# The squared-ReLU tiles of a transformer block return through the ring of weight buffers; squares of x^T queue behind q's casts

## The chip, the cores and the metric

The kernel runs on one core of a Trainium2 chip. The metric is the time of one execution in device microseconds (us), as a median of several. The core has TensorE (matmuls), VectorE (DVE), ScalarE (ACT), GpSimd (POOL) and SyncE (SP, which here only issues DMAs); 16 DMA engines move data between DRAM and the on-chip memory SBUF. Matmuls write into eight banks of PSUM.

## The reference, cut to what matters

One encoder block on 512 tokens and 16 learned meta tokens, width 2048, float32:

```python
h = rms_norm(h_res, norm1_g)
proj = h @ w_in                    # [conv B | conv C | conv x | q | k | v], 6 x 1024 columns
y_conv = short_conv_mixer(b_gate, c_gate, u, conv_w, conv_b)
y_attn = neighbourhood_attention(q, k, v, rpb)
mix = concat(rms_norm(y_conv, conv_norm_g), rms_norm(y_attn, attn_norm_g))
h_res = h_res + mix @ w_out
h = rms_norm(h_res, norm2_g)
h_res = h_res + square(relu(h @ w_up)) @ w_down     # 2048 -> 8192 -> 2048
out = rms_norm(h_res, final_norm_g)[:, 16:]
```

## The kernel before

Every float32 operand of a large product is split into two parts, hi (a cast on ACT, L182) and lo (a subtraction on DVE, L183), and each product is three matmuls: hi x hi, hi x lo, lo x hi. Weights come in slabs of 128 x 1024 (512 KB). `load` takes the next buffer of a ring (`wring["raw"]`) and lets SP issue the DMA; `slab` loads and splits into the next buffer of a second ring (`wring["split"]`). A buffer comes free when its last reader is done: a raw one after its lo part, a split one after its last matmul.

The program is written in one order, and a planner, which simulates the engines, lays each engine's instructions into a queue: by program order among those that it expects to be ready. It may move an instruction ahead of earlier ones that wait. On the chip each queue then runs strictly in its order. `tc.issue_after(i)` makes what is issued in its block stand behind `i` in the queue of `i`'s engine; it adds no wait on another engine.

**The start (L229 to L360).** x^T arrives in eight tiles `xTs`, w_in slabs for the first k and v beside it, and q's two slabs `q_raw` behind them. `split_xT` makes `h_hi` and `h_lo` from x^T times the norm's gain, 32 pieces. k and v of the first head pair are projected in two column halves (272 and 256 columns), then q (16 k steps of three 512-column matmuls, into `qps0`). The row sums of x^T squared, for the norm's scale, come from eight squares on ACT (L316) and adds on DVE (L318 to L321), read by ten one-column matmuls (L332), which stand behind q's tenth k step (`q_mid`). From these come `rst`, `diag` and `rs_bc`, whose matmuls (L354) stand behind the third step of the next k. The squares and adds stand behind the last piece of x^T (`hT_last`). The split ring of this stage gives k the first two of wp's three split buffers, and v two others; q0_0, q0_1 and k1_0 then take wp's third, first and second. wp's raw ring has three buffers.

**Up projection (L712 to L793).** 32 groups `n` of 256 hidden columns, each of four steps; a step uses one w_up slab and 42 matmuls. It multiplies in a seven-product scheme whose operands lie in `sobuf` (for the first four of eight places), in `xa_hi`, `xa_lo` and in the xc tiles. `up_out` combines the four banks on ACT and DVE into a tile `e`, one of the two halves of `xq`, applies Relu and Square on ACT, and stores it to DRAM as `a_d[n]` (L779, issued by ACT). The buffers acc0 to acc3 hold temporaries in this stage (`tsum` and the three q tiles), while the residual waits in DRAM as `acc_d`.

**Down projection (L796 to L880).** After the last up group, SBUF is given out anew: `wp2` adds two raw and three split buffers, in the space of `xa_hi` and `xa_lo`, so that the rings have five raw and six split buffers. There are eight chunks of four a tiles (each 128 x 1024, two k steps) and four column blocks `i` of 512 outputs; the last block of the last chunk is done apart (L846 to L867). A block is four slabs of w_down, and each slab feeds 24 matmuls with one a tile; so a block has 96. Each a tile is loaded from `a_d` into one of the two halves of `xq` (`AR`, L806, L819), split into one of seven places of `sobuf` (`A`), and serves all four blocks of its chunk. All four accs come back by GpSimd's queue as soon as their buffers are free (L798); `acc(i, t)` is added to at the end of each block (L840). `gF`, the final gain on all partitions (1 MB), is loaded by SP and read at the end of the last chunk's blocks (L844).

Of the kernel before, what the change touches and what calls it, by code (L numbers as in the profile page):

```python
# [99 lines left out]
def hybrid_block_kernel(  # L100
# [55 lines left out]

    def load(src, name):
        raw = wring["raw"].next(name)
        nc.sync.dma_start(raw, src)
        return raw  # L160

    def part_tiles(name):
        both = wring["split"].next(name)
        return both[:, :SLAB], both[:, SLAB:]
# [4 lines left out]
    def parts(raw, b, name):  # L169
        hi, lo = part_tiles(name)  # L170
        split(hi, lo, raw)
        return (
            hi.rearrange("p (a b) -> p a b", b=b),
            lo.rearrange("p (a b) -> p a b", b=b),
        )

    def slab(src, b, name):
        return parts(load(src, name), b, name)

    def split(hi, lo, src, scale=None):  # L180
        if scale is None:
            nc.scalar.copy(hi, src)  # L182
            nc.vector.tensor_tensor(lo, src, hi.bitcast(F32), op=ALU.subtract)  # L183
        else:
            first = nc.scalar.activation(hi, src, AF.Copy, scale=scale)
            second = nc.vector.scalar_tensor_tensor(
                lo, src, scale, hi.bitcast(F32), op0=ALU.mult, op1=ALU.subtract
            )
            return first, second

    hTp = tc.alloc_tile_pool(name="hTp", bufs=1, side="right")
    h_hi = hTp.tile([P, KT, L], F32R, name="h_hi")
# [36 lines left out]
    with tc.tile_pool(name="p0", bufs=1, side="left") as p0:  # L229
# [45 lines left out]
        def split_xT(i, q):  # L275
            n = ALL[i][0]
            cs = slice(0, n) if i == 0 else slice(L - n, L)
            for k in range(4):
                kt = 4 * q + k
                src = xTs[i][q][:, k * n : (k + 1) * n]  # L280
                both = split(h_hi[:, kt, cs], h_lo[:, kt, cs], src, scale=g1T[:, kt : kt + 1])
            return both

        k0_bank = bank("mm", "mm_k0_1")
        banks = [bank("mm", "mm_k0_0")[:, :272], k0_bank[:, :256]], out_banks(ALL, "v0")
# [8 lines left out]
                for kt in range(4 * q, 4 * q + 4):  # L294
                    project_kt(b[:1], ALL[:1], by_kt(w[a]), kt)
        for q in range(4):
            hT_last = split_xT(1, q)
        for w, b in zip(ws, banks):
            for kt in range(KT):
                project_kt(b[1:], ALL[1:], by_kt(w[kt // PER]), kt)  # L300
# [3 lines left out]
        nc.vector.tensor_copy(par, pg[:, 64:128])  # L304
        wring["split"] = Ring(*split_slots(3, wp))
        (qps0,) = out_banks(REAL, "q0", "aux")
        w_q = [parts(q_raw[a], P, f"q0_{a}") for a in range(2)]
        for kt in range(10):
            q_mid = project_kt([qps0], REAL, w_q[kt // PER], kt)


        sums = []
        with tc.issue_after(hT_last[0].ins), tc.issue_after(hT_last[1].ins):
            for i, (n, _) in enumerate(ALL):
                for q in range(4):
                    nc.scalar.activation(xTs[i][q], xTs[i][q], AF.Square)  # L316
                    if q > 0:
                        nc.vector.tensor_tensor(xTs[i][0], xTs[i][0], xTs[i][q], op=ALU.add)  # L318
                tot = xTs[i][0]
                nc.vector.tensor_tensor(tot[:, : 2 * n], tot[:, : 2 * n], tot[:, 2 * n :], op=ALU.add)  # L320
                nc.vector.tensor_tensor(tot[:, :n], tot[:, :n], tot[:, n : 2 * n], op=ALU.add)  # L321
                sums.append(tot[:, :n])
# [471 lines left out]


    accs = acc_tiles()  # L796
    for g in range(4):
        nc.gpsimd.dma_start(accs[g], acc_d[g])  # L798
    xcp.release()
    xe.release()  # L800
    xap.release()
# [1 line left out]
    wring["raw"] = Ring(*raw_slots(3, wp), *raw_slots(2, wp2))  # L803
    wring["split"] = Ring(*split_slots(3, wp), *split_slots(3, wp2))
    A = Ring(*[lambda name, i=i: part(sobuf, 2048, i) for i in range(7)])
    AR = Ring(*[lambda name, i=i: part(flat(xq), 1024, i) for i in range(2)])  # L806
    pf = ctx.enter_context(tc.tile_pool(name="pf", bufs=1, side="left"))
    gF = pf.tile([P, D], F32, name="gF")
    sq = pf.tile([P, NT, 5], F32, name="sq")
# [4 lines left out]
    turn = 0  # L814
    for ch in range(NCHUNK):
        a_hi, a_lo = [], []
        for n in range(4 * ch, 4 * ch + 4):
            r = AR.next()
            nc.sync.dma_start(r, a_d[n])  # L819
            both = A.next()  # L820
            split(both[:, 0:1024], both[:, 1024:2048], r)
            for b in range(2):
                for lst, c in ((a_hi, 0), (a_lo, 1024)):
                    lst.append([both[:, c + QUART[t // 2, b] * HT + t % 2 * P :][:, :P] for t in range(NT)])
        last = ch == NCHUNK - 1
        k0 = ch * FCH
        if last:
            nc.sync.dma_start(gF, final_g.partition_broadcast(P))
        for i in range(3 if last else 4):
            bs = [bank(tags[turn], f"d{ch}_{i}_{t}") for t in range(NT)]  # L830
            turn ^= 1
            for s_ in range(0, FCH, 2):
                wh, wl = slab(w_down[i, (k0 + s_) // 2], 512, f"dn{ch}_{i}_{s_}")
                for k in range(2):
                    kt = s_ + k
                    for t in range(NT):
                        mm3(bs[t], a_hi[kt][t], a_lo[kt][t], wh[:, k, :], wl[:, k, :], kt == 0, kt == FCH - 1)
            for t in range(NT):
                a = acc(i, t)
                nc.vector.scalar_tensor_tensor(a, bs[t], rs2[:, t : t + 1], a, op0=ALU.mult, op1=ALU.add)  # L840

                if last:
                    nc.scalar.activation(junk[t % 2], a, AF.Square, accum_out=sq[:, t, i : i + 1])
                    nc.vector.tensor_tensor(a, a, gF[:, i * 512 : (i + 1) * 512], op=ALU.mult)  # L844
# [95 lines left out]
```

## Time and profile before

| | us |
|---|---|
| runs of the kernel | 2172.78, 2173.46, 2176.41 (median 2173.46) |
| the profiled execution | 2175.9 |
| its span, first to last instruction | 2174.1 |
| TensorE busy in it | 2148.8 |
| VectorE, ScalarE, GpSimd busy | 1292.1, 798.1, 142.1 |
| mean granted clock of TensorE, as a share of full speed | 0.994 |

A row of a timeline gives an instruction's start and duration in us, its engine, its line in the code, what it writes and reads, its shape, and in brackets how long the engine was idle before it and what ended that. Adjacent like instructions are merged (x7). "SPq" is SP's queue at the moment of a DMA's issue, not the transfer. TensorE's matmuls are pipelined: the time between two starts is what one costs, not the duration shown. The granted clock is 1.00 at 2.4 GHz and near 0.5 at 1.2 GHz.

### The profile page before, as it was taken

Reading aid. Unit: us, or ns where it says so; the run is one execution under the profiler, and the core shown is the slowest. Engines: PE = TensorE matmul, PEld = TensorE weight load, DVE = VectorE, ACT = ScalarE, POOL = GpSimd, SP = SyncE. Lnnn points to the kernel's source line nnn. Section 1 sums busy time; section 2 is a strip of 40 time slices with the busy share of each in tenths; the row PEclk is TensorE's granted clock in tenths of the full one; section 3 lists DMA queues with packets and bytes.
Section 4 is the critical chain, followed back from the end, with each engine's and each line's share of the span. In section 5 each row is a group of like instructions: output and inputs, shape, how many; then the busy total and the mean of one; then the engine's idle time right before and its main releaser. Section 6 shows DMA issues by size and latency. Waiting matters only on the chain.

```text
span 2174.1 us, 33195 instructions
## 1 busy us (share of the span) xinstructions
PE 2148.8 (99%) x13660; PEld 1959.9 (90%) x13660; DVE 1292.1 (59%) x2015; ACT 798.1 (37%) x1110; POOL 142.1 (7%) x260
## 2 busy tenths in 40 slices
PE   9999999999999999999999999998999999999998
PEld 8999999999988889999999999996888888888887
DVE  6776766443435569888888888863434434434334
ACT  5454544222213334554554454442222212222223
POOL 0432311001110000000000000000000000000001
PEclk9999999999999999999999999999999999999999
DMA  5332222222253333433333433365424434333222
GB/s 188 83 93 78 83 83 79 89 96 95 90 165 111 122 126 127 136 127 136 130 134 127 136 134 119 136 260 173 136 98 134 135 98 134 118 114 125 94 87 78
DMA packets 89997, 261.32 MB, mean 120 GB/s; under 512 B 25636, under 2 KB 25716, under 8 KB 88692
## 3 DMA queue, kind: packets, MB, share of 16 engines
q1 hardware_dynamic: 84084, 234.02, 33.0%
q10 hardware_dynamic: 4608, 16.78, 1.9%
q0 software_dynamic: 1152, 8.39, 1.0%
q8 instruction: 107, 1.75, 0.3%
q14 instruction: 46, 0.38, 0.1%
HBM read 233.99 MB, written 25.17 MB: 119 GB/s over the span
## 4 chain that ended last, share of the span: by engine, by line
PE 98%; DMA 1%; ACT 0%; DVE 0%; SPq 0%; issue 0%; ACTq 0%; POOLq 0%; POOL 0%; DVEq 0%
PE d L630 10%; PE d L631 10%; PE d L632 10%; PE u L762 10%; PE u L761 10%; PE u L760 10%; PE mm_v L208 1%; PE mm_v L211 1%; PE mm_v L209 1%; PE mm_k L211 1%; PE mm_k L209 1%; PE mm_k L208 1%; PE mm_u L211 1%; PE mm_c L211 1%; PE mm_q L211 1%; PE mm_u L208 1%
## 5 line engine op out<-in xcount | busy, mean ns | idle before, releaser
L630 PE MATMUL d<-wsp_dn,sobuf 128*128 128x512 f32 x992 | 387.8, 392 | 10.7 <-ACT sobuf L182 8.5
L631 PE MATMUL d<-wsp_dn,sobuf 128*128 128x512 f32 x992 | 387.9, 391 | 0.0
L632 PE MATMUL d<-wsp_dn,sobuf 128*128 128x512 f32 x992 | 384.8, 390 | 0.0
L183 DVE TENSOR_TENSOR wsp_dn<-raw_dn,wsp_dn 128x1024 fp32r<-128x1024 f32 x124 | 151.7, 1224 | 293.0 <-ACT wsp_dn L182 293.0
L182 ACT CAST wsp_dn<-raw_dn 128x1024 fp32r<-128x1024 f32 x124 | 130.5, 1053 | 395.9 <-PE d L632 379.7
L630 PEld LDWEIGHTS d<-wsp_dn,sobuf 128*128 128x128 f32 x992 | 187.3, 189 | 50.5 <-ACT sobuf L182 8.9
L631 PEld LDWEIGHTS d<-wsp_dn,sobuf 128*128 128x128 f32 x992 | 187.4, 189 | 39.2 <-DVE wsp_dn L183 0.2
L632 PEld LDWEIGHTS d<-wsp_dn,sobuf 128*128 128x128 f32 x992 | 186.6, 188 | 38.9
L182 ACT CAST q<-raw_up 128x768 fp32r<-128x768 f32 x128 | 106.8, 834 | 237.3 <-PE u L761 167.3
L183 DVE TENSOR_TENSOR wsp_up<-tsum,wsp_up 128x1024 fp32r<-128x1024 f32 x128 | 156.4, 1222 | 49.7 <-ACT wsp_up L182 45.7
L182 ACT CAST wsp_up<-tsum 128x1024 fp32r<-128x1024 f32 x128 | 134.2, 1049 | 69.5 <-PE u L762 64.7
L760 PE MATMUL u<-sobuf,wsp_up 128*128 128x256 f32 x512 | 145.0, 283 | 0.0
L761 PE MATMUL u<-sobuf,wsp_up 128*128 128x256 f32 x512 | 145.0, 283 | 0.0
L762 PE MATMUL u<-sobuf,wsp_up 128*128 128x256 f32 x512 | 144.6, 283 | 0.0
L183 DVE TENSOR_TENSOR q<-raw_up,q 128x768 fp32r<-128x768 f32 x128 | 122.4, 956 | 34.7 <-ACT q L182 34.6
L761 PE MATMUL u<-sobuf,q 128*128 128x256 f32 x384 | 108.7, 283 | 0.0
L760 PE MATMUL u<-sobuf,q 128*128 128x256 f32 x384 | 108.5, 283 | 0.0
L762 PE MATMUL u<-sobuf,q 128*128 128x256 f32 x384 | 108.5, 283 | 0.0
L840 DVE SCALAR_TENSOR_TENSOR acc<-d,few,acc 128x512 f32<-128x512 f32 x124 | 86.7, 750 | 33.8 <-PE d L632 33.8
L760 PEld LDWEIGHTS u<-sobuf,wsp_up 128*128 128x128 f32 x512 | 98.3, 192 | 0.0
L761 PEld LDWEIGHTS u<-sobuf,wsp_up 128*128 128x128 f32 x512 | 98.3, 192 | 0.0
L762 PEld LDWEIGHTS u<-sobuf,wsp_up 128*128 128x128 f32 x512 | 98.2, 192 | 0.0
(306 smaller groups left out, 5414.9 us busy)
## 6 DMA issues: line engine op xcount, KB each, us to landing
raw_up<-in_w_up_dram SPq DMA_DIRECT2D x128, 512.0 KB
raw_dn<-in_w_down_dram SPq DMA_DIRECT2D x124, 512.0 KB
a_d<-xq ACTq DMA_DIRECT2D x32, 512.0 KB
xq<-a_d SPq DMA_DIRECT2D x32, 512.0 KB
raw_q<-in_w_in_dram SPq DMA_DIRECT2D x16, 512.0 KB
raw_u<-in_w_in_dram SPq DMA_DIRECT2D x16, 512.0 KB
raw_c<-in_w_in_dram SPq DMA_DIRECT2D x16, 512.0 KB
raw_b<-in_w_in_dram SPq DMA_DIRECT2D x16, 512.0 KB
```

The costliest lines, as they stand in the source:

```text
L182: nc.scalar.copy(hi, src)
L183: nc.vector.tensor_tensor(lo, src, hi.bitcast(F32), op=ALU.subtract)
L208: nc.tensor.matmul(b, lhsT=wh, rhs=cols(h_hi, kt), start=kt == 0, stop=False)
L209: nc.tensor.matmul(b, lhsT=wh, rhs=cols(h_lo, kt), start=False, stop=False)
L211: last = nc.tensor.matmul(b, lhsT=wl, rhs=cols(h_hi, kt), start=False, stop=kt == KT - 1)
L630: nc.tensor.matmul(o, lhsT=ah, rhs=wh, start=start, stop=False)
L631: nc.tensor.matmul(o, lhsT=ah, rhs=wl, start=False, stop=False)
L632: nc.tensor.matmul(o, lhsT=al, rhs=wh, start=False, stop=stop)
L760: nc.tensor.matmul(o, lhsT=h, rhs=xh, start=first, stop=False, skip_group_check=True)
L761: nc.tensor.matmul(o, lhsT=h, rhs=xl, start=False, stop=False, skip_group_check=True)
L762: nc.tensor.matmul(o, lhsT=l, rhs=xh, start=False, stop=m == NPR - 1, skip_group_check=True)
L840: nc.vector.scalar_tensor_tensor(a, bs[t], rs2[:, t : t + 1], a, op0=ALU.mult, op1=ALU.add)
```

## The change

Two edits. The squares and adds of x^T now stand behind the second of q's two slab splits (ACT and DVE) instead of behind the last piece of x^T. And in the down projection the a tiles are loaded by `load` into the raw weight ring, each directly ahead of the w_down slab that it is used with, in the first column block of each chunk; the ring `AR` in `xq` is gone. The four acc loads move from GpSimd's queue to SP's, one in each column block of chunk 0, behind the block's second slab. The load of `gF` stands behind the slab issued last before the last chunk.

```diff
     def load(src, name):
         raw = wring["raw"].next(name)
-        nc.sync.dma_start(raw, src)
+        wring["last"] = nc.sync.dma_start(raw, src)
         return raw
...
-        w_q = [parts(q_raw[a], P, f"q0_{a}") for a in range(2)]
+        w_q = []
+        for a in range(2):
+            hi, lo = part_tiles(f"q0_{a}")
+            q_cast = split(hi, lo, q_raw[a])
+            w_q.append(by_kt((hi, lo)))
         for kt in range(10):
             q_mid = project_kt([qps0], REAL, w_q[kt // PER], kt)
...
-        with tc.issue_after(hT_last[0].ins), tc.issue_after(hT_last[1].ins):
+        with tc.issue_after(q_cast[0].ins), tc.issue_after(q_cast[1].ins):
             for i, (n, _) in enumerate(ALL):
                 for q in range(4):
                     nc.scalar.activation(xTs[i][q], xTs[i][q], AF.Square)
...
     accs = acc_tiles()
-    for g in range(4):
-        nc.gpsimd.dma_start(accs[g], acc_d[g])
...
-    AR = Ring(*[lambda name, i=i: part(flat(xq), 1024, i) for i in range(2)])
...
     for ch in range(NCHUNK):
         a_hi, a_lo = [], []
-        for n in range(4 * ch, 4 * ch + 4):
-            r = AR.next()
-            nc.sync.dma_start(r, a_d[n])
-            both = A.next()
-            split(both[:, 0:1024], both[:, 1024:2048], r)
-            for b in range(2):
-                for lst, c in ((a_hi, 0), (a_lo, 1024)):
-                    lst.append([both[:, c + QUART[t // 2, b] * HT + t % 2 * P :][:, :P] for t in range(NT)])
...
         if last:
-            nc.sync.dma_start(gF, final_g.partition_broadcast(P))
+            with tc.issue_after(wring["last"].ins):
+                nc.sync.dma_start(gF, final_g.partition_broadcast(P))
         for i in range(3 if last else 4):
...
             for s_ in range(0, FCH, 2):
+                if i == 0:
+
+                    n = 4 * ch + s_ // 2
+                    both = A.next()
+                    split(both[:, 0:1024], both[:, 1024:2048], load(a_d[n], f"a{n}"))
+                    for b in range(2):
+                        for lst, c in ((a_hi, 0), (a_lo, 1024)):
+                            lst.append([both[:, c + QUART[t // 2, b] * HT + t % 2 * P :][:, :P] for t in range(NT)])
                 wh, wl = slab(w_down[i, (k0 + s_) // 2], 512, f"dn{ch}_{i}_{s_}")
+                if ch == 0 and s_ == 2:
+
+                    with tc.issue_after(wring["last"].ins):
+                        nc.sync.dma_start(accs[i], acc_d[i])
```

`split` now returns its two instructions in both of its branches, and `split_xT` returns nothing.

## Rows read from the trace of the kernel before

**Rows 1.** The page's busy times of the whole span (busy us, share, instructions).

```profile
PE 2148.8 (99%) x13660; PEld 1959.9 (90%) x13660; DVE 1292.1 (59%) x2015; ACT 798.1 (37%) x1110; POOL 142.1 (7%) x260
```

**Rows 2.** TensorE's waits: line, what ended them: us in total, times, longest.

```profile
PE d L630 <- ACT sobuf L182: 8.5, 1, 8.5
PE d L630 <- ACT wsp_dn L182: 2.3, 1, 2.3
PE mm_q L211 <- DVE wsp_q L183: 1.9, 1, 1.9
```

**Rows 3.** ACT's timeline around q's first cast.

```profile
24.37 6.95 ACT L316 ACTIVATE xT<-xT 128x1088 f32<-128x1088 f32 x7
31.22 1.05 ACT L182 CAST wsp_q<-raw_q 128x1024 fp32r<-128x1024 f32 x1
```

**Rows 4.** DVE's timeline: q's first lo part and the last add.

```profile
35.68 1.22 DVE L183 TENSOR_TENSOR wsp_q<-raw_q,wsp_q 128x1024 fp32r<-128x1024 f32 x1
...
41.29 0.42 DVE L321 TENSOR_TENSOR xT<-xT 128x256 f32<-128x256 f32 x1
```

**Rows 5.** TensorE's timeline: last use of k0_0, then q's first matmuls.

```profile
26.45 0.28 PE L211 MATMUL mm_k<-h_hi,wsp_k 128*128 128x256 f32 x1
...
34.30 0.50 PE L208 MATMUL mm_q<-h_hi,wsp_q 128*128 128x512 f32 x1
...
36.95 0.50 PE L211 MATMUL mm_q<-h_hi,wsp_q 128*128 128x512 f32 x1 [1.92 <-DVE wsp_q L183]
...
41.17 0.39 PE L209 MATMUL mm_q<-h_lo,wsp_q 128*128 128x512 f32 x1
```

**Rows 6.** Stretches: length, busy PE, PEld, DVE, ACT, POOL; clock; DMA share; GB/s.

```profile
26.00:28.00 2.00, 2.00 (x20) 2.00 (x19) 1.29 (x1) 2.00 (x3) 0.00 (x0) 1.00 0.00 0
...
37.50:41.20 3.70, 3.70 (x11) 2.85 (x10) 3.70 (x4) 0.00 (x0) 0.00 (x0) 0.54 0.59 173
```

**Rows 7.** TensorE's timeline: first and last d, and a stretch between.

```profile
1452.71 0.40 PE L630 MATMUL d<-wsp_dn,sobuf 128*128 128x512 f32 x1
...
1487.06 0.39 PE L631 MATMUL d<-wsp_dn,sobuf 128*128 128x512 f32 x1
...
1496.58 0.39 PE L631 MATMUL d<-wsp_dn,sobuf 128*128 128x512 f32 x1
...
2142.58 0.39 PE L630 MATMUL dl<-wsp_dlast,sobuf 128*128 128x512 f32 x1
```

**Rows 8.** The chain that ended last, at the head of the down projection: start, us.

```profile
1448.25 11.26 DMA raw_dn<-in_w_down_dram
...
1462.51 7.31 DMA a_d<-xq
1469.88 5.40 DMA xq<-a_d
```

**Rows 9.** Stretches at the head of the down projection, columns as in rows 6.

```profile
1441.00:1452.70 11.70, 11.70 (x99) 11.70 (x99) 3.60 (x3) 3.15 (x3) 1.73 (x4) 1.00 0.97 382
1452.70:1458.00 5.30, 5.30 (x26) 4.34 (x24) 4.19 (x9) 2.85 (x4) 0.00 (x0) 1.00 1.01 414
...
1460.60:1464.40 3.80, 3.78 (x10) 2.92 (x11) 3.31 (x3) 3.76 (x4) 0.00 (x0) 0.55 1.03 428
...
1467.90:1476.40 8.50, 0.05 (x1) 0.00 (x0) 2.47 (x3) 3.13 (x3) 0.00 (x0) 0.69 0.91 361
1476.40:1481.60 5.20, 5.20 (x13) 4.09 (x14) 2.24 (x2) 1.05 (x1) 0.00 (x0) 0.52 0.64 202
```

**Rows 10.** Instructions on acc from 1430 to 1500: issue to landing.

```profile
DMA to landing us min/median/max: 6.1/8.6/9.4
```

**Rows 11.** ACT's timeline: a cast that waited for a load issued at 1476.39.

```profile
1479.49 1.05 ACT L182 CAST sobuf<-xq 128x1024 fp32r<-128x1024 f32 x1 [3.14 <-DMA xq<-a_d]
```

**Rows 12.** SP's timeline: issues of w_down loads.

```profile
1438.14 0.33 SPq L159 DMA_DIRECT2D raw_dn<-in_w_down_dram  x1
...
1445.17 0.33 SPq L159 DMA_DIRECT2D raw_dn<-in_w_down_dram  x1
```

More of the change, by code (lines that the diff above doesn't have):

```diff
@@ L181, in split @@
         if scale is None:
-            nc.scalar.copy(hi, src)
-            nc.vector.tensor_tensor(lo, src, hi.bitcast(F32), op=ALU.subtract)
+            first = nc.scalar.copy(hi, src)
+            second = nc.vector.tensor_tensor(lo, src, hi.bitcast(F32), op=ALU.subtract)
         else:
@@ L188, in split @@
             )
-            return first, second
+        return first, second
     hTp = tc.alloc_tile_pool(name="hTp", bufs=1, side="right")
@@ L280, in split_xT @@
                 src = xTs[i][q][:, k * n : (k + 1) * n]
-                both = split(h_hi[:, kt, cs], h_lo[:, kt, cs], src, scale=g1T[:, kt : kt + 1])
-            return both
+                split(h_hi[:, kt, cs], h_lo[:, kt, cs], src, scale=g1T[:, kt : kt + 1])
         k0_bank = bank("mm", "mm_k0_1")
@@ L296, in hybrid_block_kernel @@
         for q in range(4):
-            hT_last = split_xT(1, q)
+            split_xT(1, q)
         for w, b in zip(ws, banks):
```

## Prediction

> **What bounds the kernel now.** I read four views, in this order. The page's busy times come first: TensorE has work in 2148.8 of 2174.1 us [rows 1], so only its few idle stretches, and the stretches at half clock, can be won. Next comes the list of waits of TensorE. It has seven entries, and three matter here: 8.5 us for a cast into sobuf, 2.3 us for a cast of a w_down slab, 1.9 us for the lo part of q's first slab [rows 2]. The other four are shorter and lie at the very start, which the change does not touch. Third, TensorE's own instructions around the three waits, and the stretches with their granted clock, because each of these waits is followed by a few us at the lower of the two clock levels. Last, ACT, DVE, SP and the chain, to see why the data was late. The tail after the last matmul stays as it is.
>
> **Part 1, the squares.** Before, ACT finishes the hi parts of x^T at 24.37 and then runs seven squares back to back, 6.95 us, ahead of q's first cast at 31.22 [rows 3]. DVE likewise runs an add of the squares ahead of q's first lo part, which starts at 35.68 and takes 1.22 [rows 4]. TensorE begins q at 34.30, needs that lo part for its third matmul, and starts it at 36.95 [rows 5]. It then runs at a granted clock of 0.54 from 37.5 to 41.2 [rows 6], that is at 1.2 instead of 2.4 GHz for nearly all of it.
> Price: the 14th matmul of q starts at 41.17, 13 steps after 34.30 [rows 5]. A step of a 512-column matmul is 0.227 us at full clock (42 steps from 1487.06 to 1496.58, [rows 7]). So the stretch took 6.87 instead of 2.95 us: 3.9 us lost, of which 1.9 idle and the rest clock.
> After: the squares and adds stand behind q's second cast and second lo part. Nothing is added. Is q's data there early enough? No DMA moved a byte between 26 and 28 us [rows 6], so both q slabs had landed by then. The first cast needs no slot of anyone (the third buffer of wp's ring is free) and runs at about 24.4 to 25.4, its lo part right after h_lo, done by about 27. The second cast needs the buffer of k0_0, whose last matmul is the 24th L211 of k's second half, at 26.45 with 0.28 duration [rows 5]: cast 26.8 to 27.9, lo part done by 29.1. q starts at 34.3, so both have 5 us to spare.
> What is late next: the sums. Eight squares (6.95/7 = 0.99 us each) from 27.9, with the cast of k1_0 among them (1.05), end at 36.8. Behind the last square follow one add (1.2, as the lo part), one over half its columns (0.7) and one over a quarter (0.42): sums at about 39.2, against 41.7 before (the last add starts at 41.29, [rows 4]). Their readers, the ten one-column matmuls, stand behind q's tenth k step, which ends at 34.3 + 30 x 0.227 = 41.1. So 1.9 us of cover remains; if that is gone, the price is the lateness, plus up to 2 us of clock. Queued behind the squares on ACT is the cast of k1, not needed before q ends (34.3 + 48 x 0.227 = 45.2). The two q raw slots come free about 9 us earlier, so SP's next loads move earlier too. Taken: -3.9; bounds -3.9 and 0 (a wait of 2 us for the sums, with 2 of clock behind it).
>
> **Part 2, the ring.** Before, the a tiles come back through the two halves of xq, in which up_out builds its own results. The second a therefore waits for the last up_out, its square, and its store: store 7.31 us from 1462.51, load 5.40 us from 1469.88, both on the chain [rows 8], and the cast that ended the 8.5 us wait [rows 2]. Beside that, the four acc loads of 1 MB and gF of 1 MB are issued into the same stretch: the 16 DMA engines are busy with share 0.97 to 1.01, a slab load on the chain takes 11.26 us [rows 8, 9], an acc load 6.1 to 9.4 [rows 10]. An undisturbed load of 512 KB lands 3.1 us after its issue: the cast at 1479.49 had waited 3.14 for it [rows 11].
> Price of the stage: the d matmuls before the last block are 31 blocks x 96 = 2976, from 1452.71 to 2142.58 [rows 7]: 689.9 us, against 2976 x 0.2267 = 674.6. So 15.3 us are lost there. The stretches say the same another way: idle 2.3 + 8.5 [rows 2], and clock (3.8 us at 0.55 and 5.2 us at 0.52, [rows 9]) 1.7 + 2.5, together 15.0. No wait of TensorE lies behind them, so all of this is the head of the down projection.
> After: a0 to a3 use weight slots and no longer see up_out. The three wp slots take a0, the first slab and a1; the third of these issues is the one at 1438.14 [rows 12]. The next two, slab 2 and a2, go into wp2, free from 1445.17 (where SP issues into it now, [rows 12]). One pair (a, slab) feeds 24 matmuls, 5.44 us. Pair 1 is needed at 1452.71 and has all its data by about 1446. Pair 2 is needed at 1458.2: slab 2 lands 3.1 to 11.3 us after 1445.2, and cast and lo part add 1.05 + 1.22, so it is ready between 1450.6 and 1458.8. Nearest is the short end, since the stretch now holds 1 MB of acc instead of 4 MB, and no gF. Pairs 3 and 4 (needed at 1463.6 and 1469.0): slab 2, acc0, a2, two slabs and a3 are 3.7 MB; at 400 GB/s (414 and 361 in two of the stretches, [rows 9]) that is 9.2 us, so all land by about 1457.5, split by 1462. Nothing else gates them: sobuf's places and the split buffers come free as the last up steps end, by 1452.7.
> The extra instructions are none: the same 32 loads, 32 casts and lo parts, four acc loads and gF, on other slots or at other times. Moved past: the four acc loads leave POOL for SP, one per column block of chunk 0, each behind the second slab; their buffers are free by then, so SP does not stop. acc0 is needed at 1474.5, 25 us after its issue. gF moves behind the last slab of chunk 6, over 40 us ahead of its first reader.
> Later heads: a's now take weight slots, so the first block of each chunk asks for 8 loads in 21.8 us from 5 slots. A slot may thus be held 5 x 21.8 / 8 = 13.6 us. Load, cast and lo part hold it 3.1 + 1.05 + 1.22 = 5.4 us undisturbed, and 11.3 + 2.3 = 13.5 at the worst load of the trace. Hidden either way, at the worst with nothing left. Taken: -15.3; bounds -15.3 and -7.3 (a wait of 2.3 us with 1.7 of clock behind it remains, twice).
>
> **Sum.** -3.9 - 15.3 = -19.2. The profiled execution took 2175.9 (span 2174.1 and 1.8 around it), so 2156.7. It lies 2.4 above the median of 2173.46; from that the sum gives 2154.3. The runs go from 2172.78 to 2176.41, so I take 2155.0.
>
> **Rivals.**
> (a) One wait of TensorE stays at the head (pair 2 or 3 late, or ACT's queue holds a cast behind one that waits for its load, as the queue order is the planner's). For it: slab 2's late end of 1458.8. Against it: four of the five MB that crowded the stretch are gone. Price: 2.3 of idle and 1.7 of clock, as at 1458 now, up to twice that: 2159 to 2163.
> (b) The sums come late: squares start 3.5 us later than now. If TensorE waits for them, part 1 gains nothing: 2159.
> (c) Slower: the ring starves at every chunk head. Decides when a slot is held over 13.6 us, against 5.4 to 13.5 from the rows. Then each of the 7 later heads costs about 4 us (2.3 idle, 1.7 clock): 2155 + 28 = 2183. Against it: away from the first head only 1 MB at a time can crowd the queue.
> (d) acc on SP's own queue: slabs line up behind it. Four transfers of 1 MB at 400 GB/s are 2.6 us each; with a full ring that is hidden, with none 4 x 2.6: 2165.
> The Trainium skill, DMA: Bandwidth & Descriptors, section Queues, rings and completion order, speaks for (d): each DMA engine takes turns between queues packet by packet, and starts one queue's work in order, so on POOL's queue acc shared the engines with the slabs, and on SP's queue it goes wholly ahead of the next. No row of the kernel before has an acc load on SP's queue.
> (e) The order does not follow the program: the planner issues the slabs first and the a's again late. Then 2170 to 2173, no change.
>
> **How the numbers follow.** Forecast 0.70 (2152 to 2158), (a) 0.11, (b) 0.07, (c) 0.04, (d) 0.04, (e) 0.04. Faster by over 0.2% (4.3 us, about what a measurement of this kernel can tell from no change) are the forecast, (a), (b) and (d): 0.92. Same: (e), 0.04. Slower: (c), 0.04. The range 2151.5 to 2162.5 takes in the forecast, (b), and most of (a), 0.87 in all by these chances; the scatter of the runs (3.6 us) takes the rest of the margin.
>
> **What would show it.** Right: no wait of TensorE over 0.3 us after 10 us; granted clock 1.00 from 30 to 66 and from 1460 to 1500; the first d matmul at about 1449, and 674.6 us from it to the last block; an a load landing before the last up_out. Wrong in part 1: TensorE waiting at L332 or L208 of k1. Wrong in part 2: TensorE waiting at L630 for a cast that waited for a load. The forecast fails as a whole if waits appear at the chunk heads, every 87 us.

## The result and the profile after

The changed kernel takes 2156.65 us in the median of four executions (2155.03 to 2158.09), the kernel before 2173.79 beside it on the same chip: ratio 0.9919, with a 95% interval of 0.9902 to 0.9936. So it is faster by 0.8%, four times the 0.2% that the prediction names as the least a measurement of this kernel can tell from no change. The profiled execution took 2155.03, its span is 2153.3. Repeated twice, the same kernel gave medians of 2155.59 and 2155.48.

First the waits of TensorE in the changed kernel: engine, line and what ended the wait; us in total, times, longest. All three long rows of [rows 2] are gone, and no row of the down projection stands in their place (its lines, 630 to 632 before, are now 633 to 635). Two short waits are new: L511 and L491 (0.32 and 0.17 us), both in the attention.

```profile
PE pg L239 <- POOL ident masks.py:199: 1.4, 1, 1.4
PE mm_k L208 <- ACT wsp_k L182: 0.9, 1, 0.9
PE yb L511 <- DVE mx L465: 0.3, 1, 0.3
PE pg L273 <- DVE g1T L271: 0.3, 1, 0.3
PE pvm L491 <- POOL pm L478: 0.2, 1, 0.2
```

TensorE's timeline in the changed kernel: q's first and 14th matmul, the first two readers of the row sums, the first d matmul and the first of the last block (start, duration). They answer to [rows 5, 7].

```profile
31.78 0.50 PE L208 MATMUL mm_q<-h_hi,wsp_q 128*128 128x512 f32 x1
...
34.91 0.39 PE L209 MATMUL mm_q<-h_lo,wsp_q 128*128 128x512 f32 x1
...
40.73 0.50 PE L335 MATMUL mm_k<-ones,xT 128*128 128x1 f32 x4
...
44.10 0.63 PE L335 MATMUL mm_k<-ones,xT 128*128 128x1 f32 x6
...
1447.41 0.40 PE L633 MATMUL d<-wsp_dn,sobuf 128*128 128x512 f32 x1
...
2122.00 0.39 PE L633 MATMUL dl<-wsp_dlast,sobuf 128*128 128x512 f32 x1
```

The stretches, with the columns of [rows 6]: length, busy PE, PEld, DVE, ACT, POOL; clock; DMA share; GB/s. TensorE is busy in the whole of each at a granted clock of 1.00, that is 2.4 GHz. The DMA engines are nearly as full at the head of the down projection as they were in [rows 9] (shares of 0.92 and 0.98), and nobody waits for that any more.

```profile
30.00:66.00 36.00, 36.00 (x224) 32.17 (x224) 26.15 (x49) 12.70 (x16) 13.53 (x22) 1.00 0.29 85
1449.00:1460.00 11.00, 11.00 (x50) 9.10 (x49) 8.20 (x12) 6.85 (x7) 0.00 (x0) 1.00 0.92 332
1460.00:1475.00 15.00, 15.00 (x68) 12.43 (x67) 6.38 (x8) 2.28 (x3) 0.00 (x0) 1.00 0.98 391
```

Where the 20.8 us between the two spans lie:

| stretch | before | after | gained |
|---|---|---|---|
| start to q's first matmul | 34.30 | 31.78 | 2.5 |
| q's first to 14th matmul | 6.87 | 3.13 | 3.7 |
| from there to the first up matmul (805.86, 800.56) | 764.69 | 765.65 | -1.0 |
| the up projection, to the first d matmul | 646.85 | 646.85 | 0.0 |
| d matmuls to the last block | 689.87 | 674.59 | 15.3 |
| the rest | 31.54 | 31.26 | 0.3 |

The first row is none of the change's: q's first matmul starts between 31.7 and 32.6 in the profiled executions of all the other kernels below, that with the old place of the squares among them (32.01), so the profiled execution of the kernel before had a late start. From 10 to 14 us its granted clock was 0.57, against 1.00 in that of the changed kernel, behind waits of TensorE of 0.65 and 0.99 us before 10 us.

### The profile page after: what moved, and what is told of

It reads as the page before. It is cut to its first block, busy times and chain, and to the rows that moved or that the text cites. A ratio compares the mean times of both kernels' runs of the same rounds, so it can differ in the third digit from the quotient of the medians.

```text
span 2153.3 us, 33207 instructions
## 1 busy us (share of the span) xinstructions
PE 2141.1 (99%) x13660; PEld 1954.4 (91%) x13660; DVE 1291.3 (60%) x2015; ACT 799.4 (37%) x1110; POOL 141.1 (7%) x256
## 4 chain that ended last, share of the span: by engine, by line
PE 98%; POOL 1%; SPq 0%; DMA 0%; ACT 0%; issue 0%; POOLq 0%; ACTq 0%; DVE 0%
PE d L633 10%; PE d L634 10%; PE d L635 10%; PE u L764 10%; PE u L765 10%; PE u L763 10%; PE mm_u L211 1%; PE mm_c L211 1%; PE mm_u L208 1%; PE mm_c L208 1%; PE mm_u L209 1%; PE mm_c L209 1%; PE mm_b L211 1%; PE mm_b L208 1%; PE mm_b L209 1%; PE o_a L635 1%
## 5 line engine op out<-in xcount | busy, mean ns | idle before, releaser
L183 DVE TENSOR_TENSOR sobuf<-raw_a,sobuf 128x1024 fp32r<-128x1024 f32 x32 | 39.2, 1225 | 103.2 <-ACT sobuf L182 103.2
L763 PEld LDWEIGHTS u<-sobuf,wsp_up 128*128 128x128 f32 x512 | 98.3, 192 | 0.0
L764 PEld LDWEIGHTS u<-sobuf,wsp_up 128*128 128x128 f32 x512 | 98.3, 192 | 0.0
```

Of the source, the lines that this page charges most:

```text
L183: second = nc.vector.tensor_tensor(lo, src, hi.bitcast(F32), op=ALU.subtract)
L763: nc.tensor.matmul(o, lhsT=h, rhs=xh, start=first, stop=False, skip_group_check=True)
L764: nc.tensor.matmul(o, lhsT=h, rhs=xl, start=False, stop=False, skip_group_check=True)
```

## The experiments

The theory: TensorE's idle time at q's start and at the head of the down projection, with the stretches at half clock behind it, was the whole of what could be won; part 1 takes the first away (3.9 us), part 2 the second (15.3), and where no wait is left, neither the number of weight buffers nor the place of the acc loads matters. The rivals: (b) the sums take the gain of part 1 back, (c) the ring starves, (d) the acc loads on SP's queue hold up the slabs, and that the gain of part 2 is not the ring's but that of the acc and gF loads leaving the stretch.

### Each part alone

The kernel before with part 1 only:

```diff
-        with tc.issue_after(hT_last[0].ins), tc.issue_after(hT_last[1].ins):
+        with tc.issue_after(q_cast[0].ins), tc.issue_after(q_cast[1].ins):
```

> Only the squares and adds behind q's second split; the a tiles, acc and gF as before. By the prediction: the 1.9 us wait at q and the stretch at 0.54 clock go, and the two waits at the head of the down projection (2.3 and 8.5 us) stay as they are: 3.7 to 3.9 us under the kernel before, about 2170. Rival (the sums come late and take the place of the wait): no gain, 2173 to 2174, with a wait of TensorE at the ten one-column matmuls.

Measured: 2170.66 (ten executions), the kernel before 2172.94 (nineteen): ratio 0.9991, interval 0.9981 to 1.0000, so 2.3 us, with 0 and 4.1 as its ends; 3.7 to 3.9 were expected. Its waits at the head of the down projection stay, and q's is gone:

```profile
PE d L634 <- ACT sobuf L182: 9.6, 1, 9.6
PE d L634 <- ACT wsp_dn L182: 3.1, 1, 3.1
```

The changed kernel with the old place of the squares (part 2 only):

```diff
-        with tc.issue_after(q_cast[0].ins), tc.issue_after(q_cast[1].ins):
+        with tc.issue_after(hT_last[0].ins), tc.issue_after(hT_last[1].ins):
```

> Only the second edit: a tiles through the raw weight ring, acc and gF later and on SP; the squares stand behind the last piece of x^T as before. By the prediction: from the first d matmul to the last block 674.6 us instead of 689.9, the wait of 1.9 us at q and its clock stay: 15.3 us under the kernel before, about 2158.5, and 3.7 over the changed kernel. If the two edits only worked together, it would lie well above that.

Measured: 2158.16, ratio 0.9930 (0.9916 to 0.9945), 14.8 us. The d matmuls to the last block take 674.59 us as in the changed kernel, and TensorE waits for q's lo part, 1.92 us as before. But in the profiled execution, the fastest of four, the stretch behind this wait is not at half clock. TensorE's timeline at the wait, then the stretch behind it:

```profile
34.66 0.50 PE L211 MATMUL mm_q<-h_hi,wsp_q 128*128 128x512 f32 x1 [1.92 <-DVE wsp_q L183]
```

```profile
34.70:37.50 2.80, 2.80 (x12) 2.30 (x13) 2.80 (x4) 0.00 (x0) 0.00 (x0) 1.00 0.56 181
```

What follows: the parts add up (2.3 + 14.8 = 17.1 by the medians; the whole change gave 17.1 to 17.3). Part 2 is worth about what was predicted. Part 1 is worth less: the same wait cost 3.7 us in the profiled execution of the kernel before, with the clock behind it at 0.54 [rows 6], and 2.2 here (q's first to 14th matmul takes 5.33 against 3.13).

### Which half of part 2 it was

The changed kernel with the acc loads back on GpSimd's queue, and gF without its place behind the last slab; the ring stays:

```diff
     accs = acc_tiles()
+    for g in range(4):
+        nc.gpsimd.dma_start(accs[g], acc_d[g])
...
-            with tc.issue_after(wring["last"].ins):
-                nc.sync.dma_start(gF, final_g.partition_broadcast(P))
+            nc.sync.dma_start(gF, final_g.partition_broadcast(P))
...
-                if ch == 0 and s_ == 2:
-                    with tc.issue_after(wring["last"].ins):
-                        nc.sync.dma_start(accs[i], acc_d[i])
```

> The changed kernel, with the four acc loads on GpSimd's queue and gF's load put back to where they were, so that 5 MB again crowd the head of the down projection; the a tiles stay in the weight ring. Theory 1 (the a tiles' way through xq behind the last up_out is what cost most; the crowd is a second, smaller cause): 0 to 4 us over the changed kernel, one wait of about 2 us at most. Theory 2 (the crowd of transfers is the cause, the a's way matters little): 10 to 15 us over it, 2167 to 2172, with waits of TensorE for slabs and a tiles whose loads take over 8 us.

Measured: 2160.93, ratio 0.9944 (0.9930 to 0.9959), 4.3 to 5.4 us above the changed kernel by the medians of its three measurements, a little over the 0 to 4 of theory 1 and far from the 10 to 15 of theory 2. In the profiled execution, the fastest of the four, the d stage (first d matmul to the last block) loses 3.0 us against the 674.6 that its matmuls take without a wait. There is one wait of TensorE in the down projection, and the chain that ended last runs through the load that it waited for (start, us, what); GpSimd issues its acc loads at 1435.92, 1437.13, 1442.17 and 1447.21, before and beside this load, gF only at 1454.36, when this load is nearly in.

```profile
PE d L633 <- ACT wsp_dn L182: 2.3, 1, 2.3
```

```profile
1443.34 11.65 DMA raw_dn<-in_w_down_dram
1455.01 1.05 ACT wsp_dn L182
```

The changed kernel with the a tiles back in the two halves of `xq`, ahead of each chunk; acc and gF stay moved:

```diff
+    AR = Ring(*[lambda name, i=i: part(flat(xq), 1024, i) for i in range(2)])
...
+        for n in range(4 * ch, 4 * ch + 4):
+            r = AR.next()
+            nc.sync.dma_start(r, a_d[n])
+            both = A.next()
+            split(both[:, 0:1024], both[:, 1024:2048], r)
...
-                if i == 0:
-                    n = 4 * ch + s_ // 2
-                    both = A.next()
-                    split(both[:, 0:1024], both[:, 1024:2048], load(a_d[n], f"a{n}"))
```

> The changed kernel with the a tiles back in the two halves of xq, loaded ahead of each chunk as before; acc and gF stay late and on SP. Theory 1: the second a still waits for the last up_out, its store and its own load; even if store and load together fall from 12.7 to about 7 us, the a is split at about 1465, while one a tile and two sets of four banks keep TensorE busy only for 10.9 us after 1447.4, to 1458.3: a wait of 5 to 7 us and about 2.5 of clock, 8 to 10 us over the changed kernel. Theory 2: without the crowd there is no wait over 1 us, 0 to 2 us over it.

Measured: 2175.94 (ten executions), ratio 1.0012 (1.0002 to 1.0021): no better than the kernel before, and 5.3 us above part 1 alone, which it contains. The direction is that of the theory, the size is not: the d stage loses 20.6 us, where 8 to 10 were expected. ACT's timeline shows why. The last up_out (L780, L781, the store L782) stands in ACT's queue behind three casts of slabs, and the first of these waits 3.90 us for its load. The chain goes through the load of the second, the store and the a load behind it.

```profile
1453.16 1.04 ACT L182 CAST wsp_dn<-raw_dn 128x1024 fp32r<-128x1024 f32 x1 [3.90 <-DMA raw_dn<-in_w_down_dram]
1454.40 1.99 ACT L182 CAST wsp_dn<-raw_dn 128x1024 fp32r<-128x1024 f32 x2 [0.20 <-DMA raw_dn<-in_w_down_dram]
1456.30 1.05 ACT L780 ACTIVATE xq<-xq 128x1024 f32<-128x1024 f32 x1
...
1459.14 1.05 ACT L781 ACTIVATE xq<-xq 128x1024 f32<-128x1024 f32 x1
1460.23 0.33 ACTq L782 DMA_DIRECT2D a_d<-xq  x1
...
1475.85 2.20 ACT L182 CAST sobuf<-xq 128x1024 fp32r<-128x1024 f32 x2 [3.99 <-DMA xq<-a_d]
```

```profile
1444.12 10.26 DMA raw_dn<-in_w_down_dram
...
1460.23 7.91 DMA a_d<-xq
1468.15 7.68 DMA xq<-a_d
```

What follows: the ring is the gain. With it alone the loss at the head falls from 15.3 to 3.0 us, and the move of acc and gF takes the last 3.0; without the ring that move gains nothing, since the a tiles still wait for up_out, which here stands behind the slab casts as well.

### Does the ring starve, does SP's order matter

The whole down projection with three raw buffers instead of five, all acc loads at once on SP behind the second slab, and two raw buffers (in the space of `xa_hi` and `xa_lo` only):

```diff
-    wring["raw"] = Ring(*raw_slots(3, wp), *raw_slots(2, wp2))
+    wring["raw"] = Ring(*raw_slots(3, wp))
```

> The changed kernel with three raw buffers in the down projection instead of five (the two of wp2 are not used). By the prediction's count a buffer may be held 3 x 21.8 / 8 = 8.2 us at the head of a chunk, and is held 5.4 us undisturbed: no wait of TensorE at the seven later heads; at the first head, where loads take up to 10 us, one wait of 1 to 3 us is possible: 0 to 5 us over the changed kernel. Rival (the ring starves at every chunk head once it is short): 2 to 4 us at each of seven heads, 14 to 28 us over it.

```diff
-                if ch == 0 and s_ == 2:
+                if ch == 0 and s_ == 2 and i == 0:
                     with tc.issue_after(wring["last"].ins):
-                        nc.sync.dma_start(accs[i], acc_d[i])
+                        for g in range(4):
+                            nc.sync.dma_start(accs[g], acc_d[g])
```

> The changed kernel with all four acc loads on SP's queue at once, behind the second slab of the first block. Theory 1 (SP's queue is served in order, so 4 MB stand ahead of the next a and slab): at 400 GB/s 10.5 us from about 1443, pair 3 is ready at about 1459 instead of 1454 and is needed at 1458.3: a wait of 1 to 3 us plus its clock, 1 to 5 us over the changed kernel. Theory 2 (only the sum of bytes in the stretch counts, which is the same as in the changed kernel, where all four are issued by 1467): 0 to 1 us over it.

```diff
-    wring["raw"] = Ring(*raw_slots(3, wp), *raw_slots(2, wp2))
+    wring["raw"] = Ring(*raw_slots(2, wp2))
```

> The changed kernel with two raw buffers for the whole down projection instead of five. In the first block of a chunk eight loads are asked for in 21.8 us, so a buffer may be held 2 x 21.8 / 8 = 5.4 us, and load, cast and lo part hold it 5.4 us undisturbed. Theory 1 (the ring starves when a buffer is held longer than that): TensorE waits in the first blocks of the chunks, over 0.3 us each at several heads, and 2160 to 2185 in all. Theory 2 (what was loaded ahead covers it; split buffers hold 6 slabs): no wait at the later heads, at most one at the first, 2155 to 2160.

Measured, with the unchanged version of the change beside them:

| kernel | us | ratio, interval | d stage loses |
|---|---|---|---|
| the change, second time | 2155.59 | 0.9923 (0.9911 to 0.9936) | 0.03 |
| three raw buffers | 2155.87 | 0.9923 (0.9910 to 0.9937) | 0.03 |
| acc at once | 2155.79 | 0.9922 (0.9907 to 0.9937) | 0.03 |
| the change, third time | 2155.48 | 0.9923 (0.9911 to 0.9936) | 0.03 |
| two raw buffers | 2163.13 | 0.9957 (0.9943 to 0.9971) | 6.3 |

With three buffers, and with 4 MB of acc at once on SP's queue (issued from 1443.72 to 1447.44), TensorE has no wait in the down projection. With two, TensorE waits three times, all between 1448 and 1465 at the first head, and at none of the seven later ones:

```profile
PE d L633 <- ACT wsp_dn L182: 4.0, 3, 2.5
```

These two buffers come free only with the end of the up projection: their first load is issued at 1443.33, where the changed kernel issues its first a load at 1422.71. So the late start and the small number act together at the first head, and the run doesn't tell them apart. The later heads do tell something. ACT's slab casts ahead of the second chunk, in the kernel with two buffers:

```profile
1521.47 1.05 ACT L182 CAST wsp_dn<-raw_dn 128x1024 fp32r<-128x1024 f32 x1 [2.89 <-DMA raw_dn<-in_w_down_dram]
...
1527.38 1.05 ACT L182 CAST wsp_dn<-raw_dn 128x1024 fp32r<-128x1024 f32 x1 [2.25 <-DMA raw_dn<-in_w_down_dram]
...
1533.26 1.05 ACT L182 CAST wsp_dn<-raw_dn 128x1024 fp32r<-128x1024 f32 x1 [2.62 <-DMA raw_dn<-in_w_down_dram]
1536.99 1.05 ACT L182 CAST wsp_dn<-raw_dn 128x1024 fp32r<-128x1024 f32 x1 [2.68 <-PE d L635]
```

A pair of a tile and slab takes 5.9 us there, more than the 5.44 that TensorE needs for one. The loads fall behind by 0.5 us a pair, 2 us in a block, and the slabs already split make up for it: by 1536.99 the cast waits for TensorE again, not for a load. Of the two theories the second is right for the later heads; the total lies above its 2155 to 2160 because of the first.

### Which half of part 1

The changed kernel with only ACT's squares behind q's casts; DVE's adds keep their old place:

```diff
-        with tc.issue_after(q_cast[0].ins), tc.issue_after(q_cast[1].ins):
+        with tc.issue_after(q_cast[0].ins), tc.issue_after(hT_last[1].ins):
```

> The changed kernel with only the squares (ACT) behind q's second cast; the adds (DVE) stand behind the last piece of x^T as before. Theory 1: what kept q's lo part late was its cast, behind seven squares on ACT; DVE takes the lo part as soon as the cast is done, so no wait at q: within 1 us of the changed kernel. Theory 2: the adds on DVE are a cause of their own: a wait of 1 to 2 us at q's third matmul.

Measured: 2155.50, ratio 0.9926 (0.9913 to 0.9938), no wait at q (first to 14th matmul 3.13 us). The adds' new place is not needed: they read the squares and so come late by themselves.

### Some executions are 3 to 4 us longer

The change once more, for its scatter:

> The changed kernel once more, with more executions and a second profile. If the first 30 us differ from one execution to the next (clock and waits there, 2.5 us between the two profiles so far), the second profile again shows the head of the down projection without a wait, and a start that may be 1 to 3 us longer or shorter; the median stays at 2155 to 2158.

Its executions: 2155.36, 2155.39, 2155.59, 2155.69 and 2159.21. The profiled one is the last. Its head of the down projection is again without a wait, as expected. Its first 30 us are only 0.5 us longer than in the first profile of the same kernel (q begins at 32.32); the long part, 3.5 us, lies elsewhere, at one place in the attention. The waits of TensorE, then GpSimd's timeline there, then the stretch behind the wait:

```profile
PE pvm L491 <- POOL pm L478: 2.1, 1, 2.1
```

```profile
78.03 4.19 POOL L445 TENSOR_TENSOR s<-bt,msk 128x64 f32<-128x64 f32 x6 [3.69 <-DMA bt<-in_attn_rpb_dram]
82.16 1.35 POOL L478 COPY pm<-s 128x32 f32<-128x32 f32 x2
```

```profile
84.50:88.50 4.00, 4.00 (x23) 4.00 (x22) 1.49 (x5) 0.99 (x5) 0.00 (x0) 0.57 0.30 119
```

GpSimd's bias adds for the second head pair wait 3.69 us for the load of the bias into `bt`, the copies of `pm` stand behind them, TensorE waits 2.1 us for these, and the clock falls to 0.57 for 4 us. In the first profile of the changed kernel the same adds waited 2.42 for the load, and TensorE 0.2 for `pm`. `bt` is one buffer, so this load cannot start before the first pair's adds are done. The wait came with part 1: with part 1 alone the same adds wait 2.44 us for the load, but in the two kernels with the squares at their old place, where the planner ordered the attention another way, they wait for TensorE's transposes (4.17 us in the kernel before; GpSimd's timeline with part 2 alone):

```profile
75.63 3.52 POOL L446 TENSOR_TENSOR s<-bt,msk 128x256 f32<-128x256 f32 x6 [4.20 <-PE yb L512]
```

To test whether this load makes the long executions, two buffers taken in turn (the second in the space of a tile used later), twice:

```diff
-        bt = at.tile([P, GR, 2, 48], F32, name="bt")
-        nc.gpsimd.memset(bt, 0.0)
+        vbb = cv.tile([P, 2 * 516], F32, name="vbb", bufs=1)
+        bts = [
+            at.tile([P, GR, 2, 48], F32, name="bt"),
+            vbb[:, 0 : GR * 96].rearrange("p (k h u) -> p k h u", h=2, u=48),
+        ]
+        for b in bts:
+            nc.gpsimd.memset(b, 0.0)
...
         for p in range(NPAIR):
+            bt = bts[p % 2]
```

> The changed kernel with two buffers bt for the bias instead of one, taken in turn by the head pairs (the second lies in the space of the conv's vb, which is not used before). The load of pair 1's bias no longer stands behind the bias adds of pair 0. Theory 1: executions near 2159 instead of 2155.5 come from GpSimd's bias adds waiting for that load (2.4 us in one profile of the changed kernel, 3.7 in the one of 2159.2), which delays GpSimd's copy of pm and so TensorE at L491. Then no bias add waits for its load here, TensorE waits under 0.3 us at L491, and all executions lie at 2154 to 2156. Theory 2: the two levels of time come from something else (start-up, clock). Then some executions still lie near 2159 although no bias add waits. The planner may lay out the attention in another order, which can shift the time by some us either way.

> The changed kernel once more, beside the other two on the same chip. Both theories: 2155 to 2156.5 as median, some executions near 2159; no wait of TensorE in the down projection. Where an execution profiled here lies near 2159, theory 1 wants a wait of 1 to 2.5 us at L491 in it, theory 2 does not.

> The kernel with two bt buffers once more, because four executions (2154.6 to 2155.3) are few: of 27 executions of the changed kernel and of its near variants without a wait in the down projection, 8 lay over 2157. Theory 1 (those come from the bias adds that wait for bt's load): all lie at 2154 to 2156, and no bias add waits for its load. Theory 2 (they come from something else): with 8 in 27, one or two of five lie over 2157.

Measured: 2154.86 (2154.58 to 2155.28, ratio 0.9918, interval 0.9904 to 0.9931) and 2154.91 (2154.85 to 2155.22, ratio 0.9912, interval 0.9898 to 0.9926); the change beside the first of them 2155.48 (2154.94 to 2157.64). GpSimd's bias adds now wait for TensorE's transposes, not for the load (its timeline in the second of these runs):

```profile
73.27 4.53 POOL L451 TENSOR_TENSOR s<-vbb,msk 128x256 f32<-128x256 f32 x6 [1.01 <-PE yb L517]
```

Of 27 executions of the change and of its variants without a wait in the down projection (three buffers, acc at once, squares on ACT only), 8 lie over 2157. Of the nine with two `bt` buffers none does; at 8 in 27 that would come about in 4 of 100 cases. That speaks for the load, but it doesn't show it: only one long execution was profiled, the nine ran on one chip, where the change has one execution over 2157 among five, and the planner laid the attention out a little differently with two buffers, so the buffer is not the only difference. The kernel with two buffers lies 0.6 us below the changed one by the medians of executions taken together; the intervals overlap, so it is not shown to be faster.

## Why the prediction was right, point by point

It said 2155.0 and faster; the median is 2156.65, later 2155.59 and 2155.48, inside the range. The gain was foreseen as 19.2 us and measured as 17.1 to 17.3; the 2 us between them are part 1's.

**What bounds the kernel** was right: with no wait left behind 10 us but two of 0.3 and 0.2, TensorE is busy in 2141.1 of 2153.3 us.

**Part 2, the size** was right to 0.1 us: 674.6 us were foreseen for the d matmuls to the last block and 674.59 measured. The first of them starts at 1447.41, near the 1449 of the prediction, in part by luck: the late start of the profile before adds 2.5 us to what part 1 moved it by, and 1.0 comes back. An a load lands before the last up_out, as it said. SP's timeline with the issues at the head, in the changed kernel:

```profile
1422.71 0.33 SPq L159 DMA_DIRECT2D raw_a<-a_d  x1
1427.74 0.33 SPq L159 DMA_DIRECT2D raw_dn<-in_w_down_dram  x1
1431.90 0.33 SPq L159 DMA_DIRECT2D raw_a<-a_d  x1
...
1442.94 0.42 SPq L838 DMA_DIRECT2D acc<-acc_d  x1
1443.41 0.43 SPq L159 DMA_DIRECT2D raw_a<-a_d  x1
1443.94 10.29 SPq L159 DMA_DIRECT2D raw_dn<-in_w_down_dram  x5
1454.28 0.42 SPq L838 DMA_DIRECT2D acc<-acc_d  x1
...
1458.13 0.64 SPq L838 DMA_DIRECT2D acc<-acc_d  x1
...
1466.74 0.36 SPq L838 DMA_DIRECT2D acc<-acc_d  x1
```

**Part 2, the steps under the size** held less well. The step "the three wp slots take a0, the first slab and a1; the third of these issues is the one at 1438.14" was off, to the good side: the third issue is at 1431.90, since a0's slot is free again after its lo part. Four of the six casts of the first three pairs have started by 1442, and a3, wanted at 1463.7, is cast at 1451.56. ACT's timeline, the casts of a0 and of a3:

```profile
1428.67 1.05 ACT L182 CAST sobuf<-raw_a 128x1024 fp32r<-128x1024 f32 x1
...
1451.56 1.05 ACT L182 CAST sobuf<-raw_a 128x1024 fp32r<-128x1024 f32 x1 [2.62 <-DMA raw_a<-a_d]
```

The step "the stretch now holds 1 MB of acc instead of 4 MB" is wrong: "one per column block" in the program is a place among the slabs, and the slabs run ahead of TensorE by the depth of the rings. So all four acc loads are issued within 24 us, and the DMA engines stay at 0.92 to 0.98 until 1475. It did no harm: a0 to a2 and the first slabs were issued ahead of them all, and a3 behind only one of them. The run with all four at once on SP shows that they need no spreading; the run with them on GpSimd's queue, issued from 8 us earlier on, shows that they can still do harm (3.0 us). Whether the queue or the earlier issue did it, these two runs don't tell apart.

**Part 1, the size** is the term that was mis-sized: 3.9 taken, 2.3 measured by part 1 alone (0 to 4.1), and 1.5 to 2.7 as the difference of the medians of the change from that of part 2 alone. Two things make it smaller. The 2 us of clock in it do not come each time: the same wait of 1.92 us stood in the profiled execution of part 2 alone with the clock at 1.00 behind it. (The other three executions of that kernel took 1.5 to 2.5 us longer; what their clock did there is not recorded.) And 1.0 us comes back between q and the up projection, in the kernel with part 1 alone as well and not in that with part 2 alone. Half of it is in the two new waits at L511 and L491, the second for `pm`, behind the load of `bt`; the other half stays open. By the profiles part 1 is thus worth 1.2 us where the clock does not fall at q (5.33 - 3.13 - 1.0) and 2.7 where it does.

**Part 1, the sums.** "Sums at about 39.2" and "1.9 us of cover" were both wrong. DVE's timeline in the changed kernel shows the last adds behind the lo parts of k1's slabs, the second of which waits for its cast:

```profile
38.73 1.23 DVE L183 TENSOR_TENSOR wsp_k<-raw_k,wsp_k 128x1024 fp32r<-128x1024 f32 x1 [1.10 <-ACT wsp_k L182]
39.88 0.69 DVE L323 TENSOR_TENSOR xT<-xT 128x512 f32<-128x512 f32 x1
40.60 0.42 DVE L324 TENSOR_TENSOR xT<-xT 128x256 f32<-128x256 f32 x1
```

The sums are done at 41.0, though the squares end 3.7 us earlier than foreseen, at 33.1. The prediction also took the readers' place from the program, behind q's tenth k step. In the kernel before only the first four, which read the sums that are done first, stand there, ahead of q's 31st matmul; the last six stand ahead of its 35th. In the changed kernel these two matmuls start at 38.85 and 39.79 (q begins 2.5 us earlier in this execution), so at the old place the last six would have waited up to 1.2 us, and at the place that the prediction took 2.2, as rival (b) had it. They do not wait, since the planner laid the rest of q's first twelve steps and k1's first matmuls, which were ready, ahead of them; they start at 44.10. So (b) was averted by the planner's order, and not by the cover that the prediction counted.

**The rivals.** (a) did not come about; it is what acc early gives (one wait of 2.3). (c) fell twice: three buffers cost nothing, two cost nothing at the later heads. Its limit, that a slot may be held 13.6 us, left out that six split buffers lie between the ring and TensorE; a ring slower than TensorE only eats into those. (d) fell with all four acc loads at once on SP. The rule cited for it (the Trainium skill, DMA: Bandwidth & Descriptors, section Queues, rings and completion order: each DMA engine takes the work of one queue in its order) agrees with the trace of that run, but the rival's price does not: the load behind three acc loads did come later, a3's cast at 1456.45 instead of 1451.56, still 8 us ahead of its use (its first d matmul being at 1448.19), so nobody waited. With acc on GpSimd's queue a slab load took 11.65 us, and TensorE waited. That agrees with the other half of the rule, that an engine takes turns between queues, but the acc loads were also issued 8 us earlier there, so the run doesn't show that the sharing did it. (e) did not happen: the a loads stand in SP's queue among the slabs, as written.

**The sum's base.** The profiled execution of the kernel before began q 1.7 to 2.6 us later than the others, and had its clock at 0.54 behind the wait at q. It lay 2.4 us above its median; no other execution of that kernel was profiled, so which of the two made the difference is not shown. Taking the sum from between the two bases rested on nothing but the scatter of the runs, and that 2155.0 lies within 1.7 us of all three medians is partly its luck: it is 18.5 below the median before, where 17.1 to 17.3 were gained.

## What to carry to other kernels

When a buffer ties the first loads of a stage to the last stores of the one before, give these loads another place before anything else is moved: here the ring without the moved acc loads left 3.0 of 15.3 us, and these moved without the ring left all of them (20.6 in that run). A loader that is a little too slow does no harm so long as a lead of finished work lies behind it and the slow stretch is shorter than the lead; count the lead before pricing a starved ring. And price a wait by its idle time, with the clock behind it as an upper end only, unless several executions show it.

## What the runs showed of the hardware that was not expected

The granted clock after a short wait of TensorE is not the same from run to run, even for the same wait in the same place. After 1.92 us of waiting at q it was 0.54 for 3.7 us in the kernel before [rows 6] and 1.00 with part 2 alone. After the first wait at the head of the down projection it was 0.55 in the kernel before (2.3 us of waiting, [rows 9]) and 1.00 with part 1 alone (3.1 us). Stretches of the latter, behind that wait and then behind its wait of 9.6 us:

```profile
1456.20:1460.00 3.80, 3.74 (x15) 2.80 (x16) 3.31 (x3) 3.73 (x4) 0.00 (x0) 1.00 1.03 428
...
1471.80:1478.00 6.20, 6.16 (x20) 4.94 (x21) 2.45 (x2) 1.66 (x2) 0.00 (x0) 0.71 0.57 170
```

The 0.71 of the second is a mean: 0.57 up to 1476, 1.00 from there. In these runs the clock fell behind all three waits of 8.5 us and more (8.5, 9.6 and 13.3), and sometimes behind those of 2 to 3 us. In the profile of the kernel before it also fell to 0.57 from 10 to 14 us, where the longest wait just before had been 0.99 us; in other profiles it stayed at 1.00 there. What decides it for the short ones stays open.

A load can take over three times its undisturbed time without any change to itself: 512 KB took 3.1 us [rows 11] in a stretch with a DMA share of 0.64 [rows 9], and 10.3 and 11.7 us with shares of 0.97 and 1.01, with acc loads of 1 MB among what was issued beside it.
